# Attention weights times values: one group of eight matmuls per head in place of two groups of four and eight

## The chip, the cores and the metric

The kernel runs on one core of a Trainium2 chip. A core has TensorE (PE in the profile; its weight loads have a row of their own, PEld), VectorE (DVE), ScalarE (ACT), GpSimd (POOL) and the DMA queues that SyncE (SP) and POOL issue. The metric is the device time of one execution in microseconds (us); the figure compared is the median over runs.

## The reference, cut to what matters

The reference is a two-layer decoder trunk on 512 tokens of width 1024, in float32. Each layer is a half-step feed-forward block, a mixer of three parallel head groups, and a second half-step feed-forward block. The change touches only the third head group, causal "forgetting" attention with 8 heads of dimension 64:

```python
def block(i):                                   # one query tile of 128 tokens
    s = einsum('bhqd,bhkd->bhqk', qb, kh) + (cb[..., :, None] - cum[..., None, :])
    s = where(qpos[:, None] >= kpos[None, :], s, MASK_VALUE)
    p = softmax(s, axis=-1)
    return einsum('bhqk,bhkd->bhqd', p, vh)     # weights times values
o = lax.map(block, arange(seqlen // 128))       # four query tiles
```

With 512 tokens there are four query tiles i and four key tiles j, and only the ten blocks with j <= i are not masked: four for j = 0, three for j = 1, two for j = 2, one for j = 3.

## The kernel before, in words

**Precision.** Float32 accuracy is kept by splitting each operand into a high part (type fp32r) and a low part, the remainder. ACT casts the high part, DVE subtracts it from the source to make the low part, and PE multiplies the parts separately.

**The layer.** `ffn`, `mix`, `ffn`, twice. Inside `mix` the attention (`fox_attend`) is a generator that is advanced step by step. Between its steps another generator, `rest`, is advanced: the last value projection, the short convolution's projections and most of the output projection. Its pieces of 9 or 12 matmuls of 512 columns (lines 451 to 458 and 536) are called "the work beside" here. The tuple `BESIDE` says how many pieces go before each attention step. Nearly all PE instructions of this stage are tied into one chain (`follow("p", ...)`; in `fox_attend` the helper `E` does this), so PE's order is the order of the program text. ACT's and DVE's order in the attention is left to the framework's scheduler, which takes ready instructions in the order of the text.

**Steps.** `steps` runs over (head h, p) with h = 0..7 and p = 0, 1, where p = 0 means query tiles 0 and 1 and p = 1 means query tiles 2 and 3. So a layer has 16 steps; the even-numbered ones have p = 0. In step k the kernel runs, in this order:

- `turn(h, p)` transposes the step's weight blocks on PE (line 1843; 3 blocks for p = 0, 7 for p = 1) into PSUM banks "pt", casts the high parts on ACT (1848, tile PH) and subtracts the low parts on DVE (1849, tile PL). Each step has its own PH and PL of seven blocks, two buffers each.
- For p = 0, `prep(h + 2)` transposes and splits a later head's queries and keys (1769 to 1780).
- `scores(steps[k + 2])` writes mask and query-key products into the PSUM banks "sc" (1804), then takes row maxima on DVE (1820), exponentials on ACT (340), a reciprocal (1822) and the scaling to weights (1826 on ACT, 1828 on DVE). There are two "sc" banks, used in turn: p = 0 takes one and p = 1 takes two, so the second bank that a p = 1 step writes is the one that the p = 0 step before it used.
- `values(steps[k - 1])` multiplies the previous step's turned blocks with the head's values V (1861). V holds a head's high and low part side by side, so the 128 output rows are 64 rows of products with the high part and 64 with the low part. The output goes to the single PSUM bank "po".

For p = 0 `values` runs four matmuls: key tile 0 with 256 columns and key tile 1 with 128, each for PH and PL. For p = 1 it runs eight: key tiles 0, 1, 2 with 256 columns and key tile 3 with 128. After p = 1 ACT copies the lower 64 rows out (1874) and DVE adds the upper 64 (1880; for the last head also 1879). The sums feed the last two rows of the output projection, at the end of the stage (line 559 and the lines around it).

Of the kernel before, what the change touches and what calls it, by code (L numbers as in the profile page):

```python
# [9 lines left out]
F32R = mybir.dt.float32r  # L10
# [17 lines left out]
P = 128  # L28
# [35 lines left out]

SKEW_HELD, SKEW_MOVING = 16, 48
EPS = 1e-6
CH = 64
NCH = T // CH
HD = 64
NH = 8  # L70
# [140 lines left out]
class Trunk:  # L211
# [8 lines left out]
    def __init__(self, ctx, tc):  # L220
# [25 lines left out]
        self.epsc = self.const.tile([P, 1], F32, tag="epsc", name="epsc")  # L246
        nc.vector.memset(self.epsc, EPS)
        self.xT = self.res.tile([P, KD, T], F32, tag="xT", name="xT")
# [3 lines left out]
    def build_consts(self, scratch):  # L252
# [16 lines left out]
        nc.vector.memset(self.smask, 1.0)  # L269
        nc.vector.memset(self.smask.rearrange("p (c t) -> p c t", t=CH)[:, :, 0:1], 0.0)  # L270
        self.identb = c.tile([P, P], BF16, tag="identb", name="identb")
# [3 lines left out]

        self.lmask = c.tile([P, 6, CH], U8, tag="lmask", name="lmask")
        self.same = c.tile([P, CH], F32, tag="same", name="same")
        ft = scratch(I32)[:, :P]
# [6 lines left out]
        for i in (  # L285
# [3 lines left out]
            self.tc.add_manual_dep(i.ins, self.first_rows, NOSYNC, reason="opening order")  # L289
        xf = scratch(F32)[:, :CH]  # L290
        later = scratch(F32)[:, : P + CH]
        later, own = later[:, :P], later[:, P:]
# [328 lines left out]
    def rsqrt(self, out, v, r, t):  # L621
# [4 lines left out]
            ("v", nc.vector.scalar_tensor_tensor(  # L626
                out=t, in0=v, scalar=EPS, in1=t, op0=ALU.add, op1=ALU.mult
            )),
# [1154 lines left out]
    def fox_attend(self, pool, half, g):  # L1783


        nc = self.nc
        tl = lambda tag, n: pool.tile([P, T], F32, tag=tag, name=self.n(tag), bufs=n)
        E = lambda i: self.follow("p", i)
        ops, weights, turned = {}, {}, {}

        def prep(h):
            ops[h] = self.fox_prep(pool, h, half[h // 4], g)

        def scores(h, p):
            QA, QB, KA, KB = ops[h]
            pb = pool.tile([P, (384, 896)[p]], F32, tag=f"P{p}", name=self.n("P"), bufs=2)
            s2 = lambda tag: pool.tile([P, 2], F32, tag=tag, name=self.n(tag), bufs=2)
            nm, rs = s2("nm"), s2("rs")
            if p == 0:
                b = self.bank("sc")  # L1800
                at = [b[:, :P], b[:, P : 3 * P]]
            else:
                at = [self.bank("sc")[:, : 3 * P], self.bank("sc")]
            mm = lambda *a, **k: E(nc.tensor.matmul(*a, skip_group_check=True, **k))  # L1804
            if p == 0:
                masked = [b.rearrange("p (b t) -> p b t", t=P)[:, ::2, :]]
            else:
                masked = [at[u][:, (2 + u) * P : (3 + u) * P] for u in range(2)]
            for m in masked:
                mask = self.maskb.unsqueeze(1).to_broadcast([P, 2, P]) if p == 0 else self.maskb  # L1810
                mm(m, self.identb, mask, start=True, stop=False)
            for u in range(2):
                i = 2 * p + u
                c, n = slice(i * P, (i + 1) * P), (i + 1) * P
                mm(at[u], QA[:, c], KA[:, :n], start=False, stop=False)
                mm(at[u], QB[:, c], KB[:, :n], start=False, stop=True)
            to = [pb[:, :P], pb[:, P:]] if p == 0 else [pb[:, : 3 * P], pb[:, 3 * P :]]
            for u in range(2):
                o = slice(u, u + 1)
                nc.vector.tensor_reduce(nm[:, o], at[u], axis=AX.X, op=ALU.max, negate=True)  # L1820
                self.act(to[u], at[u], AF.Exp, bias=nm[:, o], accum_out=rs[:, o])
            nc.vector.reciprocal(rs, rs)
            for u in range(2):
                o = slice(u, u + 1)
                if p:
                    nc.scalar.activation(to[u], to[u], AF.Copy, scale=rs[:, o])
                else:
                    nc.vector.tensor_scalar(to[u], to[u], scalar1=rs[:, o], scalar2=None, op0=ALU.mult)
            weights[h, p] = to

        def turn(h, p):


            to = weights.pop((h, p))
            blocks = [(j, u) for j in range(2 * p + 2) for u in range(2) if j <= 2 * p + u]
            PH, PL = (
                pool.tile([P, 7, P], F32R, tag=t_, name=self.n(t_), bufs=2) for t_ in ("PH", "PL")
            )
            for a in range(0, len(blocks), 4):
                some = blocks[a : a + 4]  # L1840
                tb = self.bank("pt")
                for k, (j, u) in enumerate(some):
                    E(nc.tensor.transpose(
                        tb[:, k * P : (k + 1) * P], to[u][:, j * P : (j + 1) * P], self.ident
                    ))
                ph, pl = (x[:, a : a + len(some), :].rearrange("p b t -> p (b t)") for x in (PH, PL))
                t = tb[:, : len(some) * P]
                nc.scalar.copy(ph, t)
                nc.vector.tensor_sub(pl, t, ph)
            turned[h, p] = blocks, PH, PL  # L1850

        def values(h, p):
            blocks, PH, PL = turned.pop((h, p))
            if p == 0:
                self.ob = self.bank("po")
            last = 2 * p + 1
            for j in range(last + 1):
                at = [k for k, (jj, _) in enumerate(blocks) if jj == j]
                o = slice((2 * p + 2 - len(at)) * P, (2 * p + 2) * P)
                for part in (PH, PL):  # L1860
                    E(nc.tensor.matmul(
                        self.ob[:, o], half[2][:, j, h].rearrange("p a d -> p (a d)"),
                        part[:, at[0] : at[-1] + 1, :].rearrange("p b t -> p (b t)"),
                        start=j == 0 and part is PH, stop=j == last and part is PL,
                        skip_group_check=True,
                    ))
            if p == 0:
                return
            r = slice(64 * (h % 2), 64 * (h % 2) + 64)
            if h % 2 == 0:  # L1870
                self.fo = tl("fo", 1)
            fo = self.fo
            ft = tl(self.tt, self.tb)
            nc.scalar.copy(ft[r, :], self.ob[64:, :])
            if h == NH - 1:

                kt = 4 + h // 2
                nc.scalar.copy(self.yh[kt][:64, :], fo[:64, :])
                nc.vector.tensor_add(self.yh[kt][r, :], self.ob[:64, :], ft[r, :])
            nc.vector.tensor_add(fo[r, :], self.ob[:64, :], ft[r, :])  # L1880
            if h % 2:
                kt = 4 + h // 2
                if h < NH - 1:
                    nc.scalar.copy(self.yh[kt], fo)
                nc.vector.tensor_sub(self.yl[kt], fo, self.yh[kt])

        steps = [(h, p) for h in range(NH) for p in range(2)]
        prep(0)
        yield
        scores(0, 0)  # L1890
        prep(1)
        yield
        scores(0, 1)
        yield
        for k, (h, p) in enumerate(steps):
            turn(h, p)
            if p == 0 and h + 2 < NH:
                prep(h + 2)
            if k + 2 < len(steps):
                scores(*steps[k + 2])  # L1900
            if k:
                values(*steps[k - 1])
            yield
        values(*steps[-1])


    def turn_x(self, res, banks):
# [136 lines left out]
```

## Time and profile before

| | |
|---|---|
| median of 3 runs | 1750.8 us (1749.13 to 1750.95) |
| profiled execution, span from first to last instruction | 1747.5 us |
| PE busy | 1742.1 us, 100% of the span |
| DVE busy | 1415.7 us, 81% |
| ACT busy | 1015.0 us, 58% |
| the values matmuls (line 1861) | 192, with 192 weight loads |
| steps of the attention, layer 0 | 459.5 to 548 us |
| steps of the attention, layer 1 | 1323 to 1411 us |

No separate time of the profiled execution is given beyond its span; the median lies 3.3 us above the span.

How to read the rows: a matmul's duration in the trace holds the pipeline's depth, so a row of 0.28 us may stand for an instruction that holds PE for 0.12 us. What an instruction takes from a busy PE is the distance from its start to the next one's start. In the timeline the columns are the start, the duration, the engine, the line, the operation, output<-inputs, the shape (rows * columns of the held operand, then the moving operand's shape), and the count; a bracket is idle time and what ended it.

### The profile page before, as it was taken

How to read it: one execution, taken by the hardware profiler on the slowest of the kernel's cores; microseconds unless marked ns; L12 is line 12 of the kernel's file. 1: busy time of each engine (PE TensorE's matmuls, PEld its weight loads, DVE VectorE, ACT ScalarE, POOL GpSimd, SP SyncE). 2: the span in 40 equal slices, each digit the busy share in tenths (PEclk: the TensorE clock that was granted, in tenths of full speed). 3: DMA queues.
4: the chain of work that ended last, by engine and by line, in shares of the span. 5: the costliest groups of instructions: out<-in, count | busy, mean ns of one | idle time of the engine just before them, and what ended most of it. 6: DMA issues, size and time to landing. Idle time of an engine off the chain costs nothing.

```text
span 1747.5 us, 33342 instructions
## 1 busy us (share of the span) xinstructions
PE 1742.1 (100%) x13615; PEld 1643.9 (94%) x13615; DVE 1415.7 (81%) x1907; ACT 1015.0 (58%) x1406; POOL 177.0 (10%) x174
## 2 busy tenths in 40 slices
PE   9999999999999999999999999999999999999999
PEld 7999999888888999999989999998888989999998
DVE  7988788678787898888688888876878779888793
ACT  5565565465766565566455656555657665655652
POOL 0011120100000112012001111201000000120200
PEclk9999999999999999999999999999999999999999
DMA  7768784243542876868277787923445447787762
GB/s 213 190 144 194 189 173 107 73 127 92 140 124 89 234 164 152 210 158 170 85 197 165 179 185 180 186 74 80 109 109 144 115 127 196 163 180 190 166 137 97
DMA packets 257449, 262.34 MB, mean 150 GB/s; under 512 B 25816, under 2 KB 236512, under 8 KB 257296
## 3 DMA queue, kind: packets, MB, share of 16 engines
q1 hardware_dynamic: 201440, 192.02, 37.1%
q0 software_dynamic: 55840, 68.19, 24.3%
q8 instruction: 107, 1.75, 0.4%
q14 instruction: 46, 0.38, 0.1%
q10 hardware_dynamic: 16, 0.00, 0.0%
HBM read 226.15 MB, written 2.17 MB: 131 GB/s over the span
## 4 chain that ended last, share of the span: by engine, by line
PE 95%; DVE 2%; issue 2%; DMA 1%; ACT 0%; POOL 0%; SPq 0%; DVEq 0%; POOLq 0%; ACTq 0%
PE mm L451 11%; PE mm L458 11%; PE mm L457 11%; PE mm L536 9%; PE pt L451 6%; PE pt L457 6%; PE pt L458 6%; PE sc L458 6%; PE sc L451 6%; PE sc L457 6%; PE po L451 3%; PE po L457 3%; PE po L458 3%; PE po L536 2%; PE sc L1804 1%
## 5 line engine op out<-in xcount | busy, mean ns | idle before, releaser
L964 DVE TENSOR_TENSOR hl<-w,hl 128x1024 fp32r<-128x1024 f32 x279 | 340.9, 1223 | 89.8 <-ACT hl L962 88.2
L962 ACT CAST hl<-w 128x1024 fp32r<-128x1024 f32 x279 | 293.0, 1050 | 198.0 <-PE mm L458 55.3
L438 DVE TENSOR_TENSOR hl<-st,hl 128x1024 fp32r<-128x1024 f32 (+3 forms) x152 | 159.7, 1053 | 97.4 <-ACT hl L432 96.5
L432 ACT CAST hl<-st 128x1024 fp32r<-128x1024 f32 (+3 forms) x151 | 137.3, 912 | 147.8 <-PE po L458 40.0
L458 PE MATMUL mm<-xc,hl 128*128 128x256 f32 x696 | 191.6, 275 | 0.1
L451 PE MATMUL mm<-xc,hl 128*128 128x256 f32 x698 | 191.6, 275 | 0.0
L457 PE MATMUL mm<-xc,hl 128*128 128x256 f32 x696 | 191.5, 275 | 0.0
L451 PE MATMUL pt<-xc,hl 128*128 128x256 f32 x546 | 149.7, 275 | 0.0
L457 PE MATMUL pt<-xc,hl 128*128 128x256 f32 x544 | 149.7, 275 | 0.0
L458 PE MATMUL pt<-xc,hl 128*128 128x256 f32 x544 | 149.6, 275 | 0.0
L458 PEld LDWEIGHTS mm<-xc,hl 128*128 128x128 f32 x696 | 133.6, 192 | 0.5 <-DVE hl L964 0.5
L451 PEld LDWEIGHTS mm<-xc,hl 128*128 128x128 f32 x698 | 133.9, 192 | 0.1
L457 PEld LDWEIGHTS mm<-xc,hl 128*128 128x128 f32 x696 | 133.6, 192 | 0.0
L451 PE MATMUL sc<-xc,hl 128*128 128x256 f32 (+1 forms) x466 | 127.8, 275 | 0.7 <-DVE u L1085 0.7
L458 PE MATMUL sc<-xc,hl 128*128 128x256 f32 x464 | 127.8, 275 | 0.0
L457 PE MATMUL sc<-xc,hl 128*128 128x256 f32 x464 | 127.7, 275 | 0.0
L536 PE MATMUL mm<-hl,x 128*128 128x512 f32 x432 | 107.4, 384 | 0.0
L451 PEld LDWEIGHTS pt<-xc,hl 128*128 128x128 f32 x546 | 104.7, 192 | 0.0
L457 PEld LDWEIGHTS pt<-xc,hl 128*128 128x128 f32 x544 | 104.4, 192 | 0.0
L458 PEld LDWEIGHTS pt<-xc,hl 128*128 128x128 f32 x544 | 104.4, 192 | 0.0
L451 PE MATMUL mm<-x,hl 128*128 128x512 f32 x272 | 104.4, 384 | 0.0
L458 PE MATMUL mm<-x,hl 128*128 128x512 f32 x272 | 103.1, 379 | 0.0
(529 smaller groups left out, 5464.6 us busy)
## 6 DMA issues: line engine op xcount, KB each, us to landing
w<-in_ffn_w_in_dram SPq DMA_DIRECT2D x124, 512.0 KB, 5.4
w<-in_ffn_w_out_dram POOLq DMA_DIRECT2D x50, 512.0 KB, 9.7
w<-in_ffn_w_out_dram SPq DMA_DIRECT2D x49, 512.0 KB, 4.4
st<-in_ffn_w_out_dram SPq DMA_DIRECT2D x39, 512.0 KB, 3.6
st<-in_w_mix_in_dram SPq DMA_DIRECT2D x72, 256.0 KB, 3.1
st<-in_ffn_w_in_dram SPq DMA_DIRECT2D x71, 256.0 KB, 3.3
w<-in_ffn_w_in_dram POOLq DMA_DIRECT2D x29, 512.0 KB, 9.3
w<-S POOLq DMA_DIRECT2D x29, 512.0 KB, 5.1
```

Source lines behind the costliest of these rows:

```text
L432: a = nc.scalar.copy(hi, src[:, c : c + w])
L438: b = nc.vector.tensor_sub(lo, src[:, c : c + w], hi)
L451: i = nc.tensor.matmul(acc[:, c], ah, bh[:, c.start // 2 : c.stop // 2, :], start=first and c.start == 0, stop=False, skip_group_check=True,)
L457: nc.tensor.matmul(acc, ah, bl, start=False, stop=False, skip_group_check=True)
L458: i = nc.tensor.matmul(acc, al, bh, start=False, stop=last, skip_group_check=True)
L536: self.follow("p", self.nc.tensor.matmul(acc, *((w, woven(x)) if toks is None else (x[:, toks], woven(w))), start=k == 0 and id(acc) not i ...
L962: A(nc.scalar.copy(hi, src))
L964: return lambda: V(nc.vector.tensor_sub(lo, src, hi))
L1804: mm = lambda *a, **k: E(nc.tensor.matmul(*a, skip_group_check=True, **k))
```

## The change

Each head now has one PH and one PL tile of ten blocks, allocated in the p = 0 step, one buffer each. The blocks are ordered by key tile, and within a key tile by query tile in the order 0, 2, 3, 1 (`COLUMNS`), so that the blocks of one key tile are contiguous and their output columns are contiguous in PSUM: 512 columns for key tile 0, 384 for key tile 1, 256 for key tile 2, 128 for key tile 3. `values` runs once per head with eight matmuls instead of twice with four and eight. It runs at the start of the next head's p = 0 step, ahead of that step's `turn`, no longer behind `scores`; the p = 1 steps have no `values`.

`turn` makes the same transposes, and the same number of casts and subtractions with the same sizes, but groups the blocks differently (3; 4 and 3) and writes them with strides into the ten-block tile. Since the output columns stand in the order 0, 2, 3, 1, each final add is split into two adds of 256 columns that put them back in order.

```diff
+COLUMNS = (0, 2, 3, 1)
+PLACES = tuple((j, i) for j in range(4) for i in COLUMNS if i >= j)
+TURNS = (
+    (((0, 0), (0, 1), (1, 1)),),
+    (((0, 2), (0, 3), (1, 2), (1, 3)), ((2, 2), (2, 3), (3, 3))),
+)
...
-            blocks = [(j, u) for j in range(2 * p + 2) for u in range(2) if j <= 2 * p + u]
-            PH, PL = (
-                pool.tile([P, 7, P], F32R, tag=t_, name=self.n(t_), bufs=2) for t_ in ("PH", "PL")
-            )
-            for a in range(0, len(blocks), 4):
-                some = blocks[a : a + 4]
+            if p == 0:
+                turned[h] = [
+                    pool.tile([P, 10, P], F32R, tag=t_, name=self.n(t_)) for t_ in ("PH", "PL")
+                ]
+            for some in TURNS[p]:
                 tb = self.bank("pt")
...
+                at = [PLACES.index(x) for x in some]
+                t = tb[:, : len(some) * P].rearrange("p (b t) -> p b t", t=P)
+                if len(at) == 4:
+                    t = t.rearrange("p (j b) t -> p j b t", b=2)
+                    ph, pl = (
+                        x[:, at[0] : at[0] + 6].rearrange("p (j b) t -> p j b t", b=3)[:, :, :2]
+                        for x in turned[h]
+                    )
+                else:
+                    ph, pl = (x[:, at[0] : at[-1] + 1 : at[1] - at[0]] for x in turned[h])
                 nc.scalar.copy(ph, t)
                 nc.vector.tensor_sub(pl, t, ph)
...
+        def values(h):
+            parts = turned.pop(h)
+            self.ob = self.bank("po")
+            for j in range(4):
+                at = [n for n, (jj, _) in enumerate(PLACES) if jj == j]
+                o = COLUMNS.index(PLACES[at[0]][1])
+                for part in parts:
                     E(nc.tensor.matmul(
-                        self.ob[:, o], half[2][:, j, h].rearrange("p a d -> p (a d)"),
-                        part[:, at[0] : at[-1] + 1, :].rearrange("p b t -> p (b t)"),
-                        start=j == 0 and part is PH, stop=j == last and part is PL,
+                        self.ob[:, o * P : (o + len(at)) * P],
+                        half[2][:, j, h].rearrange("p a d -> p (a d)"),
+                        part[:, at[0] : at[-1] + 1].rearrange("p b t -> p (b t)"),
+                        start=j == 0 and part is parts[0], stop=j == 3 and part is parts[1],
                         skip_group_check=True,
                     ))
...
+            def add(to):
+                for n, b in ((0, slice(0, 4, 3)), (2, slice(1, 3))):
+                    three = lambda x: x.rearrange("p (b t) -> p b t", t=P)
+                    nc.vector.tensor_add(
+                        three(to)[:, n : n + 2], three(self.ob[:64, :])[:, b], three(ft[r, :])[:, b]
+                    )
...
-                nc.vector.tensor_add(self.yh[kt][r, :], self.ob[:64, :], ft[r, :])
-            nc.vector.tensor_add(fo[r, :], self.ob[:64, :], ft[r, :])
+                add(self.yh[kt][r, :])
+            add(fo[r, :])
...
         for k, (h, p) in enumerate(steps):
+            if p == 0 and h:
+                values(h - 1)
             turn(h, p)
             if p == 0 and h + 2 < NH:
                 prep(h + 2)
             if k + 2 < len(steps):
                 scores(*steps[k + 2])
-            if k:
-                values(*steps[k - 1])
             yield
-        values(*steps[-1])
+        values(NH - 1)
```

More of the change, by code (lines that the diff above doesn't have):

```diff
@@ L1841, in turn @@
+            for some in TURNS[p]:
                 tb = self.bank("pt")
-                for k, (j, u) in enumerate(some):
+                for k, (j, i) in enumerate(some):
                     E(nc.tensor.transpose(
-                        tb[:, k * P : (k + 1) * P], to[u][:, j * P : (j + 1) * P], self.ident
+                        tb[:, k * P : (k + 1) * P], to[i - 2 * p][:, j * P : (j + 1) * P], self.ident
                     ))
-                ph, pl = (x[:, a : a + len(some), :].rearrange("p b t -> p (b t)") for x in (PH, PL))
@@ L1847, in turn @@
-                t = tb[:, : len(some) * P]
+                at = [PLACES.index(x) for x in some]
[8 more added lines that the diff above has]
+                    ph, pl = (x[:, at[0] : at[-1] + 1 : at[1] - at[0]] for x in turned[h])
@@ L1848, in turn @@
                 nc.scalar.copy(ph, t)
                 nc.vector.tensor_sub(pl, t, ph)
[L1850 to L1860, printed above, removed]
+        def values(h):
[5 more added lines that the diff above has]
+                for part in parts:
@@ L1865, in values @@
+                        start=j == 0 and part is parts[0], stop=j == 3 and part is parts[1],
                         skip_group_check=True,
                     ))
-            if p == 0:
-                return
             r = slice(64 * (h % 2), 64 * (h % 2) + 64)
```

## The prediction

> **What bounds the kernel now.** I read the page first (busy shares, clock, chain), then the attention's PE timeline, then the DVE and ACT timelines at the places where PE's order would change.
>
> ```profile
> PE 1742.1 (100%) x13615; PEld 1643.9 (94%) x13615; DVE 1415.7 (81%) x1907; ACT 1015.0 (58%) x1406; POOL 177.0 (10%) x174
> PEclk9999999999999999999999999999999999999999
> PE 95%; DVE 2%; issue 2%; DMA 1%; ACT 0%; POOL 0%; SPq 0%; DVEq 0%; POOLq 0%; ACTq 0%
> ```
>
> PE is busy all the time at full granted clock, and the chain that ends last is 95% PE. So the kernel's time is PE's instruction stream: whatever leaves that stream leaves the time, unless PE then waits. A window of layer 0's attention says the same of the stage: 26.00 us of 26.00 for PE, while DVE and ACT have room.
>
> ```profile
> core 0: us, PE busy (x) PEld busy (x) DVE busy (x) ACT busy (x) POOL busy (x), PEclk, DMA share, GB/s
> 455.00:481.00 26.00, 26.00 (x160) 23.32 (x159) 18.42 (x39) 19.12 (x43) 1.55 (x3) 1.00 0.51 132
> ```
>
> **What the values matmuls cost now.** The next fence is the PE timeline of one head: first the p = 0 group and the work beside behind it, then the p = 1 group.
>
> ```profile
> 475.09 0.29 PE L1861 MATMUL po<-PH,V 128*128 128x256 f32 x1
> ...
> 475.51 0.43 PE L451 MATMUL mm<-x,hl 128*128 128x512 f32 x1
> 475.78 0.38 PE L457 MATMUL mm<-x,hl 128*128 128x512 f32 x1
> ...
> 477.94 0.38 PE L458 MATMUL mm<-x,hl 128*128 128x512 f32 x1
> ...
> 479.50 0.28 PE L1861 MATMUL po<-PH,V 128*128 128x256 f32 x1
> 479.62 0.28 PE L1861 MATMUL po<-PL,V 128*128 128x256 f32 x1
> ...
> 480.21 0.22 PE L1861 MATMUL po<-PH,V 128*128 128x128 f32 x1
> 480.27 0.27 PE L1861 MATMUL po<-PL,V 128*128 128x128 f32 x1
> 480.38 0.43 PE L451 MATMUL mm<-x,hl 128*128 128x512 f32 x1
> 480.65 0.38 PE L457 MATMUL mm<-x,hl 128*128 128x512 f32 x1
> ```
>
> Read the starts. A 256-column matmul takes 0.12 us (479.50 to 479.62). The two of 128 columns are marked 0.06 and 0.11 apart, but the 512-column matmul behind them then takes 0.27 us (480.38 to 480.65) where the next ten take 0.216 each (475.78 to 477.94): PE is still waiting for weights there. So the pair really costs 0.06 + 0.11 + 0.05 = 0.22 us, 0.11 each. That 128 columns cost nearly as much as 256 says that below some 0.11 us the weight load is the limit, not the columns. A head costs (475.78 - 475.09 - 0.216) + (480.65 - 479.50 - 0.216) = 0.474 + 0.934 = 1.41 us (0.216 is the 512-column matmul's own).
>
> **What they cost after.** The columns are the same (2560 a head); four matmuls and four weight loads go, two of them of the 128-column kind that pays for a load. The trace holds the new shapes in the same order elsewhere: `fox_decay` multiplies fp32r parts from contiguous rows, 512, 384, 256, 128 columns, each twice, into one bank.
>
> ```profile
> 390.11 0.39 PE L1669 MATMUL pt<-utri,flh 128*8 128x512 f32 x1
> 390.34 0.40 PE L1669 MATMUL pt<-utri,fll 128*8 128x512 f32 x1
> 390.58 0.33 PE L1669 MATMUL pt<-utri,flh 128*8 128x384 f32 x1
> 390.75 0.33 PE L1669 MATMUL pt<-utri,fll 128*8 128x384 f32 x1
> 390.92 0.28 PE L1669 MATMUL pt<-utri,flh 128*8 128x256 f32 x1
> 391.04 0.28 PE L1669 MATMUL pt<-utri,fll 128*8 128x256 f32 x1
> 391.15 0.22 PE L1669 MATMUL pt<-utri,flh 128*8 128x128 f32 x1
> ```
>
> Pairs: 0.47 us for 512 columns, 0.34 for 384, 0.23 for 256. Their held operand has only 8 columns, so no 128-column load limits them; for the last pair I therefore take the 0.22 us measured above, and 0.24 for the 256 pair, as line 1861 itself has it. Sum 0.47 + 0.34 + 0.24 + 0.22 = 1.27 us. The gain is 1.41 - 1.27 = 0.14 us a head, over 16 heads **2.2 us**.
>
> Bounds. From above: if the new matmuls ran like the work beside (0.216 for 512 columns and in proportion 0.162 and 0.108), a head costs 0.43 + 0.32 + 0.22 + 0.22 = 1.19 and 0.22 x 16 = 3.5 us go. From below: the slowest long matmuls of the stage are those of the scores,
>
> ```profile
> 474.62 0.39 PE L1804 MATMUL sc<-A 128*128 128x512 f32 x1
> 474.85 0.40 PE L1804 MATMUL sc<-kb,kb 66*128 66x512 f32 x1
> ```
>
> 0.23 and 0.24 us (474.62 to 474.85 to 475.09); with 0.24, 0.18, 0.12 and 0.11 a head costs 1.30 and 1.8 us go. I take `fox_decay`'s price: contiguous operand and shapes are the nearest.
>
> [...]
>
> **The parts that move or grow.** Transposes, casts and subtractions stay as many and as large; strides on blocks of 128 contiguous elements I cost at nothing, between -0.05 and +0.05 us each on ACT and DVE, where neither bounds the stage. The final add becomes two:
>
> ```profile
> L1849 DVE TENSOR_TENSOR PL<-pt,PH x48: 536/557/692, 460.6 to 1409.0; 128x384 fp32r<-128x384 f32 x32, 128x512 fp32r<-128x512 f32 x16
> L1880 DVE TENSOR_TENSOR fo<-po,t x16: 673/683/685, 472.7 to 1413.7; 64x512 f32<-64x512 f32 x16
> ```
>
> 128 columns are worth 692 - 557 = 135 ns, so a 256-column add is about 683 - 270 = 0.41 us and the two 0.82: +0.14 us on DVE for each of 18 adds, 2.5 us in all, hidden in DVE's idle quarter (18.42 busy of 26.00 us). At the stage's end the output projection's own work stands ahead of the last head's result, and the values' end moves later together with that work; I cost it at nothing.
>
> No DMA is added or moved on SP or POOL; `prep`'s six small DMAs stay behind the same transposes, which come 0.8 us later in the even steps (1.27 ahead of them, 0.47 gone).
>
> **Waits.** Values now stand first in an even step, nearer to their PL. The tightest place is step 1 to step 2 of each layer:
>
> ```profile
> 466.55 1.15 DVE L1849 TENSOR_TENSOR PL<-pt,PH 128x512 fp32r<-128x512 f32 x2
> ...
> 468.24 0.49 PE L1843 MATMUL pt<-ident,P 128*128 128x128 f32 x3
> ```
>
> PL is done at 467.70. PE would begin the values at 468.24 less the 0.47 us group gone from step 1, at 467.77: just after it, and PL is first needed by the second matmul, 0.23 us later. No wait. One buffer for PH and PL makes none either: their next writers wait for transposes that PE runs behind the values.
>
> The place that does get tight is the second "sc" bank of a p = 1 step. Between the scores of an even step and those of the odd one 0.93 us of values disappear. In steps 2 and 4 of each layer only one piece of work beside (12 matmuls) stands between, in nearly all later steps two or 18 matmuls (`BESIDE`); the fence has step 2, with ACT's copy as it falls now:
>
> ```profile
> 472.10 0.58 ACT L1874 COPY t<-po 64x512 f32<-64x512 f32 x1
> 472.11 0.43 DVE L1820 TENSOR_REDUCE nm<-sc 128x1 f32<-128x256 f32 x1 [0.53 <-ACT P L340]
> 472.71 0.47 ACT L340 ACTIVATE P<-sc,nm 128x256 f32<-128x256 f32 x1
> 474.10 0.28 PE L1804 MATMUL sc<-maskb,identb 128*128 128x128 bf16 x2
> ```
>
> The bank's last reader ends at 473.18, the mask matmul starts at 474.10: 0.92 us of room. In the new order PE arrives at 474.10 - 0.47 (step 1's group) - 0.93 (this step's group) + 1.27 (the new group, now ahead) = 473.97. Before the last reader now come the copy (0.58 us on ACT) and the adds (0.82 us on DVE), which came behind or between. If the engines' idle time takes them in, such as the 0.53 us in front of the reduction, the reader still ends by 473.5 and nothing waits; if DVE's adds are passed on in full, it ends at 474.00; if copy and adds are both passed on, at 474.58 and PE waits 0.6 us. So 0 to 0.6 us a place, nothing below zero. I take 0.1, because the middle case lands within 0.03 us of PE; at four places (steps 3 and 5, two layers) **0.4 us**.
>
> **Sum.** -2.2 + 0.4 = -1.8 us on a span of 1747.5: 1745.7, and with the 3.3 us that the median has beyond the span 1749.0 us. A measurement of this kernel can tell about 0.2%, 3.5 us, from no change; so this is a small gain inside that.
>
> **The rivals.**
>
> A, the forecast: 2.2 us of PE work gone, tenths given back, 1747.3 to 1750.8. Chance 0.46.
>
> B, slower: the "sc" bank's wait decides. Place: the mask matmul of the p = 1 scores in steps 3 and 5 of both layers; everything on PE queues behind it. If DVE puts, beside the adds, one long subtraction of the work beside ahead of the reduction,
>
> ```profile
> 474.62 1.23 DVE L438 TENSOR_TENSOR hl<-st,hl 128x1024 fp32r<-128x1024 f32 x1 [0.56 <-ACT hl L432]
> ```
>
> the reader ends at 474.58 + 1.23 = 475.81 and PE waits 1.84 us a place, 7.4 in all: 1750.8 - 2.2 + 7.4 = 1756.0. The kernel is slower than before from 0.56 us a place, and by over 0.2% from 1.43. For it: DVE and ACT work in turns on this chain, and their order is the scheduler's. Against it: the subtraction waits for its own cast, and DVE idles 7.6 us of 26. [...] Chance 0.27, of which 0.15 beyond 0.2%.
>
> C, clearly faster: the long matmuls run at the work beside's rate and no bank waits: -3.5 us. The scores of step 2 also have a hitch, in each layer, of 0.27 - 0.11 = 0.16 us that a later start may remove,
>
> ```profile
> 469.12 0.30 PE L1804 MATMUL sc<-A 128*128 128x128 f32 x1
> 469.39 0.30 PE L1804 MATMUL sc<-kb,kb 66*128 66x128 f32 x1
> ```
>
> another 0.3: 1747.0. For it: 512 columns do take 0.216 us in the work beside. Against it: in `fox_decay` they do not. [...] Chance 0.23.
>
> D, nothing: the loads are hidden after all and only columns count, which are equal. 1750.8. Against it speak the 0.27 us rows. Chance 0.04.
>
> **How the numbers follow.** The predicted time is A's, 1749.0. Faster by over 0.2% is C, 0.23; slower is B's far part, 0.15; within is the rest, 0.46 + 0.12 + 0.04 = 0.62. The range takes in C to 1746.0 and B up to 1754.3, which leaves out B's far part and a little below, under 0.2. A's own range is 1747.3 to 1750.8.
>
> **What would show it.** Line 1861: 128 matmuls instead of 192; starts within a head 0.235, 0.17, 0.12 apart; a head 1.27 us. DVE: 36 adds of about 0.41 us. PE gaps, if any, before line 1804 in steps 3 and 5. I am wrong if line 1861's matmuls wait for PL, if the mask matmul waits more than 0.5 us, or if the reordered ACT and DVE delay the casts of the work beside.

## The result and the profile after

The changed kernel takes 1756.0 us (median of 5 runs, 1753.64 to 1757.28) against 1749.15 us for the kernel before in the same comparison: the ratio is 1.0034, 95% interval 1.0023 to 1.0045. It is slower, by 6.85 us from median to median (5.8 from mean to mean), where a gain of 1.8 us was forecast, and its time lies above the stated range. The kernel before lies 1.65 us under the 1750.8 that the prediction started from. Lines of the changed file stand 8 lower in the helpers and some 18 lower behind the attention; in the rows below L1872 is the values matmul, L1812 the scores, L1828 the row maxima, L348 the exponentials, L1884 the copy, L1889 the adds.

The page of the changed kernel, busy shares and the chain by engine:

```profile
PE 1743.1 (99%) x13551; PEld 1642.8 (94%) x13551; DVE 1414.3 (81%) x1925; ACT 1015.9 (58%) x1406; POOL 177.1 (10%) x174
PE 93%; DVE 4%; ACT 1%; issue 1%; DMA 1%; SPq 0%; ACTq 0%; DVEq 0%
```

There are 64 matmuls and 64 weight loads fewer, as the change says. But PE's share has fallen to 99% and 5% of the chain now run over DVE and ACT: PE waits. Its waits in the changed kernel, longest first (total us, times, longest):

```profile
PE sc L1812 <- ACT P L348: 6.8, 6, 1.9
PE po L1984 <- PEq L2047: 0.8, 1, 0.8
PE pt L1849 <- DVE b L1781: 0.5, 2, 0.3
```

The first row is new, and larger than the 4.5 us that even the shortest run lost: six times, in steps 3, 5 and 9 of each layer, the scores' mask matmul waits for an exponential (0.36, 1.86 and 1.18 us in layer 0; 0.33, 1.86 and 1.18 in layer 1). The second is the start of the kernel, 0.8 us before and after; the third is a short wait of step 3's transposes. What the merged group itself costs, in the PE timeline of one head:

```profile
478.46 0.40 PE L1872 MATMUL po<-PH,V 128*128 128x512 f32 x1
478.69 0.39 PE L1872 MATMUL po<-PL,V 128*128 128x512 f32 x1
478.92 0.34 PE L1872 MATMUL po<-PH,V 128*128 128x384 f32 x1
479.10 0.34 PE L1872 MATMUL po<-PL,V 128*128 128x384 f32 x1
479.27 0.28 PE L1872 MATMUL po<-PH,V 128*128 128x256 f32 x1
479.40 0.28 PE L1872 MATMUL po<-PL,V 128*128 128x256 f32 x1
479.52 0.22 PE L1872 MATMUL po<-PH,V 128*128 128x128 f32 x1
479.57 0.28 PE L1872 MATMUL po<-PL,V 128*128 128x128 f32 x1
479.69 0.51 PE L1849 MATMUL pt<-ident,P 128*128 128x128 f32 x3
```

From 478.46 to 479.69 are 1.23 us, and some 0.02 us more show in the transposes behind. Against 1.41 us before, 0.16 us a head and 2.5 us in all left PE's stream. They were more than given back here, in step 5 of layer 0 (PE timeline):

```profile
484.41 0.22 PE L1812 MATMUL sc<-maskb,identb 128*128 128x128 bf16 x1
486.49 0.22 PE L1812 MATMUL sc<-maskb,identb 128*128 128x128 bf16 x1 [1.86 <-ACT P L348]
```

The first mask goes into the p = 1 step's own bank; the second needs the bank that step 4's scores still hold, and stands for 1.86 us. What DVE did meanwhile, from the end of step 4's values at 479.8 on:

```profile
481.47 0.75 DVE L1889 TENSOR_TENSOR fo<-po,t 64x256 f32<-64x256 f32 x2 [2.04 <-ACT t L1884]
482.25 0.56 DVE L1863 TENSOR_TENSOR PL<-pt,PH 128x384 fp32r<-128x384 f32 x1
482.73 0.74 DVE L1781 SCALAR_TENSOR_TENSOR b<-pt,qkg,b 128x512 fp32r<-128x512 f32 x1
483.39 0.68 DVE L1903 TENSOR_TENSOR fyl<-fo,fyh 128x512 fp32r<-128x512 f32 x1
483.99 0.28 DVE L1828 TENSOR_REDUCE nm<-sc 128x1 f32<-128x128 f32 x1
484.19 0.68 DVE L1396 TENSOR_TENSOR cu<-mm,iv 128x512 f32<-128x512 f32 x1
484.79 0.42 DVE L1828 TENSOR_REDUCE nm<-sc 128x1 f32<-128x256 f32 x1
```

and ACT:

```profile
479.60 1.24 ACT L1834 ACTIVATE P<-P,rs 128x384 f32<-128x384 f32 x2
480.86 0.58 ACT L1884 COPY t<-po 64x512 f32<-64x512 f32 x1
...
484.30 0.37 ACT L348 ACTIVATE P<-sc,nm 128x128 f32<-128x128 f32 x1 [1.27 <-DVE nm L1828]
484.57 0.19 ACT L348 ACTIVATION_READ_ACCUMULATOR P<-sc,nm 128x1 f32 x1
484.66 0.82 ACT L440 CAST hl<-st 128x768 fp32r<-128x768 f32 x1
485.38 0.59 ACT L1862 CAST PH<-pt 128x512 fp32r<-128x512 f32 x1
485.86 0.48 ACT L348 ACTIVATE P<-sc,nm 128x256 f32<-128x256 f32 x1
```

Read them as one chain. The values are done at 479.8, but ACT is busy with two scalings until 480.8 and copies only then. DVE's next instruction is the adds, which need the copy, so DVE stands still for 2.04 us. Five instructions (the two adds and three others) then pass before the first maximum at 483.99, although step 4's scores were complete at about 481.2. The second maximum follows only after the first exponential has begun and something of the work beside (L1396) is put in between; the second exponential then stands behind two casts on ACT. It ends at 486.3, and PE has been at the mask since 484.4.

The profiled run (1757.28 us) has one more part. In two stretches of 3.4 us PE's granted clock is half (0.50 from 1260.2 to 1263.2 and from 1355.8 to 1358.8), one of them right behind the wait of 1.86 us in layer 1:

```profile
core 0: us, PE busy (x) PEld busy (x) DVE busy (x) ACT busy (x) POOL busy (x), PEclk, DMA share, GB/s
1354.00:1355.50 1.50, 1.06 (x6) 0.97 (x6) 1.50 (x5) 1.38 (x4) 0.00 (x0) 1.00 0.86 204
1355.50:1359.00 3.50, 3.50 (x11) 2.75 (x10) 3.27 (x7) 1.50 (x5) 0.57 (x1) 0.52 0.35 114
```

In that stretch the work beside's matmuls start 0.43 us apart (1355.99, 1356.42, 1356.84), behind it 0.216 (1359.22 to 1360.30); eight of them make 1.7 us, an estimate from these starts. Two of the five runs have a mean clock of 0.998 and take 1757.0 and 1757.3 us; the two shortest have 1.000 and take 1753.6 and 1753.8. The median run, 1756.0, has 1.000 too, so the clock does not explain all of the spread. The balance of the profiled run against the span of before is: waits 6.8 + 0.5, half clock 3.4, merging -2.5, and one wait of 0.7 us for a DVE result in the second feed-forward block that the profiled run of before had and this one has not: +7.5 of the 8.0 us that the spans differ by.

### The profile page after: what moved, and what is told of

Read it like the earlier page. It is cut to its first block, busy times and chain, and to the rows that moved or that the text cites. A ratio compares the mean times of both kernels' runs of the same rounds, so it can differ in the third digit from the quotient of the medians.

```text
span 1755.5 us, 33238 instructions
## 1 busy us (share of the span) xinstructions
PE 1743.1 (99%) x13551; PEld 1642.8 (94%) x13551; DVE 1414.3 (81%) x1925; ACT 1015.9 (58%) x1406; POOL 177.1 (10%) x174
## 4 chain that ended last, share of the span: by engine, by line
PE 93%; DVE 4%; ACT 1%; issue 1%; DMA 1%; SPq 0%; ACTq 0%; DVEq 0%
PE mm L459 10%; PE mm L466 10%; PE mm L465 10%; PE mm L544 9%; PE pt L459 6%; PE pt L465 6%; PE pt L466 6%; PE sc L466 6%; PE sc L459 6%; PE sc L465 6%; PE po L459 3%; PE po L465 3%; PE po L466 3%; PE po L544 2%; PE sc L1812 1%
```

## The experiments

Theory W: merging gains about 2.4 us of PE time, and what is lost is the wait for the second "sc" bank, made by the order in which ACT and DVE now work. Rival S: the new tile's shape (strided casts, one buffer, split adds) is at fault. Rival D: only the distance on PE between two scores groups, from which 0.93 us of values went. "Before" in the tables is the kernel before on the same chip as the run.

| kernel | median us | before us | ratio (95%) | PE's wait at the scores, us (times) |
|---|---|---|---|---|
| the change | 1756.0 | 1749.15 | 1.0034 (1.0023 to 1.0045) | 6.8 (6) |
| e1 merged, behind the scores | 1751.1 | 1749.99 | 1.0007 (0.9998 to 1.0016) | 0.5 (2) |
| e2 copy and adds behind the scores | 1755.9 | 1749.99 | 1.0035 (1.0022 to 1.0048) | 0.5 (2) |
| e3 before, values first | 1758.26 | 1749.99 | 1.0050 (1.0037 to 1.0062) | 6.1 (6) |
| e4 before, split adds | 1749.67 | 1749.99 | 1.0001 (0.9992 to 1.0010) | none |
| e5 change, second mask later | 1750.36 | 1749.27 | 1.0004 (0.9996 to 1.0013) | 1.4 (2) |
| e6 e2, but head 3 early | 1754.49 | 1749.27 | 1.0029 (1.0020 to 1.0039) | 4.3 (4) |
| e7 e6 with e5's mask | 1752.08 | 1749.27 | 1.0014 (1.0005 to 1.0023) | 3.0 (2) |
| e8 change, copy on DVE | 1751.08 | 1749.27 | 1.0011 (1.0002 to 1.0020) | 3.8 (4) |
| e9 change, both maxima first | 1747.78 | 1749.51 | 0.9986 (0.9977 to 0.9995) | none |
| e10 e9 with e8's copy | 1750.07 | 1749.51 | 1.0003 (0.9994 to 1.0012) | 2.6 (2) |
| e11 before, both maxima first | 1749.5 | 1749.51 | 1.0000 (0.9991 to 1.0008) | none |

### e1: the merged group behind the scores

```diff
-            if p == 0 and h:
-                values(h - 1)
             turn(h, p)
+            if p:
+                split(h, p)
...
                 scores(*steps[k + 2])
+            if p == 0:
+                if h:
+                    values(h - 1)
+                split(h, p)
```

`split` is the half of `turn` with the casts and subtractions; for p = 0 it has to come behind `values`, because the ten-block tile has a single buffer.

> The merged group of eight matmuls is kept, with the ten-block tile, the strided writes and the split adds; it stands behind the step's scores, where the old p = 1 group stood, and the p = 0 step's casts into the single-buffered tile come behind it. Theory W (the loss is the wait for the second sc bank, made by moving the values and their copy and adds ahead of the scores): no PE wait at the scores' mask matmul, the 0.15 us a head of PE work stay gained, 1749.2 - 2.4 = 1746.8 us, between 1746 and 1748. Rival S (the new tile makes it slow: strided casts, one buffer, two adds instead of one): 1753 or more, as the changed kernel. Rival D (only the 0.93 us that no longer stand between two scores groups on PE count): 1746.8, since the distance is back.

Measured 1751.1 us: neither 1746.8 nor 1753. The bank's wait is nearly gone with the whole new tile in place, which speaks against S, but the 2.4 us were not kept. PE's waits of this kernel behind the start:

```profile
PE mm L544 <- ACT cyh L1416: 0.7, 2, 0.4
PE pt L1847 <- DVE rs L1830: 0.5, 2, 0.3
PE sc L1812 <- ACT P L348: 0.5, 2, 0.2
```

In place of one large wait there are several small ones, for a cast of the work beside, for a reciprocal, for the bank (the two waits left at the scores are at an even step's bank, not at the second bank of a p = 1 step). My theory had only the bank; it missed that ACT and DVE have other due times as tight. These waits are not the whole difference. The first matmul on the tile `m` (line 457, here 465), ahead of all that was changed, starts at 104.52 us in this profiled run and at 102.88 before; in e2 it is 105.53 and in e3 104.92. No run here says why.

### e2: matmuls first, copy and adds behind the scores

```diff
             if k + 2 < len(steps):
                 scores(*steps[k + 2])
+            if p == 0 and h:
+                finish(h - 1)
```

`finish` is the part of `values` behind the matmuls.

> The changed kernel with its eight matmuls first in the step, as they are; only the copy and the adds (and what follows from them) are written behind the scores. Theory W, with the order of ACT and DVE as the cause: the mask matmul waits at most 0.2 us a place, 1747.0 to 1748.5 us. Rival D (the lost distance on PE alone): the waits stay near 4 us a layer, 1753.6 to 1757. Rival S: the same as the changed kernel, 1753.6 to 1757.

Measured 1755.9 us, the figure that D and S named; but the trace says why:

```profile
PE mm L544 <- ACT fyh L1904: 3.9, 2, 2.0
PE po L1989 <- PEq L2052: 0.8, 1, 0.8
PE sc L1812 <- ACT P L348: 0.5, 2, 0.3
```

PE's order, and so the distance, is the changed kernel's, and the bank's wait fell from 6.8 to 0.5 us. So D falls, and so does S: the order of ACT and DVE made that wait. W had the wait right and the time (1747.0 to 1748.5) wrong: the time did not fall, because now the output projection waits 2 us in each layer for head 3's cast, whose copy and adds were put off, and four of the five runs have a mean clock of 0.998, where all of e1's have 1.000: 0.2% of the profiled run's 1755.7 us is 3.5 us, by estimate two stretches of 1.7 us.

### e3: the kernel before with its groups first

```diff
+            if k:
+                values(*steps[k - 1])
             turn(h, p)
...
-            if k:
-                values(*steps[k - 1])
```

> The kernel before, with its two groups of four and eight matmuls, its two buffers and its single adds, but each group moved to the start of its step. Theory W: no PE work is gained; the copy and the add stand ahead of the reductions as in the changed kernel, and the four-matmul group still gives 0.47 us of distance, so the waits are those of the changed kernel less 0.47 us each: about 0.1, 1.5 and 0.9 us a layer, 5 us in all, 1754 us (1752 to 1756). Rival S: 1749, nothing of the tile is changed. Rival D: 1749, since 0.92 and 0.80 us of room cover the 0.46 us of distance lost.

```profile
PE sc L1804 <- ACT P L340: 6.1, 6, 1.7
```

Six waits, the longest 1.73 us where 1.5 was expected, with not one matmul merged and nothing of the tile changed. S and D expected 1749. The time, 1758.3, is above W's 1752 to 1756, in which it was already counted that no PE work is saved. The profiled run and three others have a mean clock of 0.998, which W did not count, but the median run has 1.000, so part of the excess stays open.

### e4: the split adds alone

```diff
-            nc.vector.tensor_add(fo[r, :], self.ob[:64, :], ft[r, :])
+            for c in (slice(0, 2 * P), slice(2 * P, 4 * P)):
+                nc.vector.tensor_add(fo[r, c], self.ob[:64, c], ft[r, c])
```

> The kernel before with each final add done as two adds of 256 columns, nothing else. Theory W and rival D: 1749 us, within 1 us, since DVE has room where the adds stood. Rival S: slower by 2 us or more, 1751 and up.

1749.67 against 1749.99: nothing, as W and D expected. S is out for the adds too.

### e5: the second mask later

```diff
-            for m in masked:
+            for m in masked[:1]:
...
             for u in range(2):
+                if p and u:
+                    mm(masked[1], self.identb, self.maskb, start=True, stop=False)
```

> The changed kernel; in a p = 1 step the mask matmul into the second sc bank stands behind the first bank's two products, not ahead of them, so PE reaches that bank 0.44 us later (264 + 180 ns, the two products of 384 columns). Theory W: every wait before that mask gets shorter by up to 0.44 us (0.36 to 0, 1.86 to 1.4, 1.18 to 0.75 us, twice), 2.4 us less: 1753.5 us, between 1751 and 1755, and what is left still ends with an exponential before that mask. Rival (PE waits there for something else that merely shows as the bank, such as the first bank or the operands): waits and time unchanged, 1755 to 1757.

```profile
PE sc L1812 <- ACT P L348: 1.4, 2, 0.7
```

1750.4 us, below the 1751 to 1755 that W gave. The two waits left are those of step 9, 0.69 us each, which is 1.18 less 0.49, as the dose says; ACT's and DVE's order there is the changed kernel's. In step 5 the wait went altogether, where 1.4 us should have stayed. There the scheduler also put the copy ahead of the two scalings (480.59 and 481.20 in its ACT timeline), so that DVE stood still for 0.44 us before the adds, not 2.04, and the second exponential ahead of the casts of PH, where the change has it behind one. So a reorder of 0.44 us on PE moved the other engines' order as well, and the experiment is no pure dose.

### e6 and e7: head 3's result early, then also the mask later

```diff
             if p == 0 and h:
                 values(h - 1)
+                if h == 4:
+                    finish(3)
...
-            if p == 0 and h:
+            if p == 0 and h and h != 4:
                 finish(h - 1)
```

> The second experiment (eight matmuls first, copy and adds behind the scores), but for head 3 alone, whose result the output projection takes up in the same step, copy and adds stand right behind the matmuls. Theory: the projection's wait of 1.95 us for head 3's cast goes in both layers, and the bank's wait in step 9 comes back (about 1.2 us), the waits in steps 3 and 5 stay below 0.5 us: 1755.9 - 3.9 + 2.4 = 1754.4, or down to 1751 if the half-clock stretches behind the 1.95 us waits (1.7 us each) go too. Rival (late adds are bad for another reason than that deadline): 1755 to 1757 as in the second experiment.

> The sixth experiment with the fifth's later mask. Theory: the wait in step 9 falls by 0.44 us in both layers and those in steps 3 and 5 go, about 1.5 us less than the sixth: 1750 to 1752. If the parts do not add up, because ACT and DVE then fall behind elsewhere, it stays with the sixth.

```profile
PE sc L1812 <- ACT P L348: 4.3, 4, 1.9
```

That row is e6's. The projection's wait for head 3 is gone in both layers, which confirms the due time, and the bank's wait in step 9 is back with 1.9 us (1.2 expected); 1754.5 us as forecast. In e7 step 9's wait is 1.5 us, the others are gone, 1752.1 us, just above what was forecast. (One of e7's eleven runs took 3658 us; nothing here gives a reason. The median of the other ten is 1751.8.) For step 8 there is thus no good place in the text as long as the maxima stand apart: adds early make the bank late, adds late make the projection late.

### e8: the copy on DVE

```diff
-            nc.scalar.copy(ft[r, :], self.ob[64:, :])
+            nc.vector.tensor_copy(ft[r, :], self.ob[64:, :])
```

> The changed kernel with the copy of the lower 64 rows on DVE in place of ACT, so that DVE's adds no longer wait for ACT's queue (2.04 us idle in step 4, 1.31 in step 8). Theory W in its form 'DVE stands still behind a copy that is late on ACT': adds start 1.3 us sooner and cost 0.68 us more, the waits in steps 5 and 9 fall by about 0.7 us: 1756 - 3 = 1753 (1751 to 1755). Rival 'DVE has too much work': one more DVE instruction of 0.68 us a head makes the waits longer, 1757 or more.

```profile
PE sc L1812 <- ACT P L348: 3.8, 4, 1.1
```

DVE has 0.7 us a head more to do and the kernel is 5 us faster than the change, at the lower edge of the forecast. So too much work on DVE was not the trouble. Step 5's wait fell from 1.86 to 0.76 us and step 3's went, which fits DVE standing behind a copy that was late on ACT; step 9's stayed at 1.13 us where a fall of 0.7 was expected, so there the copy alone does not decide.

### e9 to e11: both maxima before both exponentials

```diff
             for u in range(2):
                 o = slice(u, u + 1)
                 nc.vector.tensor_reduce(nm[:, o], at[u], axis=AX.X, op=ALU.max, negate=True)
+            for u in range(2):
+                o = slice(u, u + 1)
                 self.act(to[u], at[u], AF.Exp, bias=nm[:, o], accum_out=rs[:, o])
```

e9 is the changed kernel with this alone, e10 has e8's copy besides, e11 is the kernel before with this alone.

> The changed kernel with one change in the scores: both row maxima stand ahead of both exponentials, so that on DVE the second reduction of a p = 0 step follows the first at once and nothing long comes between them. Values, copy and adds stay first in the step. Theory (the bank is late because its second reduction waits for the first exponential and lets adds, casts and the work beside pass): the bank's last reader ends 0.6 to 1.5 us sooner, the waits in steps 3 and 9 go, that in step 5 is at most 0.7 us; 0 to 1.4 us left over both layers, 1749.3 - 2.4 + (0 to 1.4) = 1746.9 to 1748.3 us. Rival (the moved values starve DVE and ACT as a whole, whatever their order): the waits only move, 1751 or more.

> The ninth with the copy on DVE as in the eighth. If the ninth has already no wait left, the added 0.68 us a head on DVE does nothing or harms: 1747 to 1749. If the ninth still waits for ACT's copy in step 5, this is faster than the ninth by up to 1.4 us.

> The control: the kernel before with both row maxima ahead of both exponentials, nothing else. PE waits for no bank there, so theory: unchanged, 1749.3 within 1 us. If this alone is faster by 2 us, the ninth's gain is not the merging's.

e9 takes 1747.78 us: faster than the changed kernel and than the kernel before (0.9986, interval 0.9977 to 0.9995). Its DVE in the stretch that was shown for the changed kernel, step 4 of layer 0:

```profile
480.56 0.75 DVE L1891 TENSOR_TENSOR fo<-po,t 64x256 f32<-64x256 f32 x2 [0.60 <-ACT t L1886]
481.34 0.62 DVE L1828 TENSOR_REDUCE nm<-sc 128x1 f32<-128x128 f32 x2
482.33 0.69 DVE L1905 TENSOR_TENSOR fyl<-fo,fyh 128x512 fp32r<-128x512 f32 x1 [0.37 <-ACT fyh L1904]
```

its ACT, and all its waits on PE:

```profile
479.95 0.58 ACT L1886 COPY t<-po 64x512 f32<-64x512 f32 x1 [0.18 <-PE pt L1851]
480.56 1.23 ACT L1836 ACTIVATE P<-P,rs 128x384 f32<-128x384 f32 x2
...
483.28 0.37 ACT L348 ACTIVATE P<-sc,nm 128x128 f32<-128x128 f32 x1
483.53 0.21 ACT L348 ACTIVATION_READ_ACCUMULATOR P<-sc,nm 128x1 f32 x1
483.62 0.48 ACT L348 ACTIVATE P<-sc,nm 128x256 f32<-128x256 f32 x1
```

```profile
PE po L1986 <- PEq L2049: 0.8, 1, 0.8
PE sc L465 <- DVE m L900: 0.2, 1, 0.2
```

The maxima stand together (x2) right behind the adds, the exponentials follow each other on ACT, the last reader ends at 484.1 instead of 486.3, and no wait at the scores is left. The values and the adds are those of the changed kernel, and so is PE's order. In step 4, however, the scheduler moved a second thing: the copy stands ahead of the two scalings, and DVE stood still for 0.60 us, not 2.04. So for step 5's wait e9 does not separate the two orders, and e5 (with its mask 0.44 us later) and e2, which have the copy ahead of the scalings but the maxima apart, wait there only 0 and 0.26 us. Step 9's wait is the clean case. In step 8 the copy follows the scalings in both kernels, DVE's idle time before the adds is 1.31 us in both and the first maximum comes 3.13 us behind the copy's start in both; only the second maximum now follows at once, and the wait of 1.18 us is gone.

e11, the control, is 1.0000: the order of the maxima alone is worth nothing where PE does not wait for the bank, so what e9 gains over before comes with the merging. Of the 2.5 us saved, 1.7 reached the median. The profiled runs show 1.2 of it where the change is: from `fox_decay`'s first matmul to the first matmul on `xc` behind the attention (390.11 to 600.23 us before) e9 is 0.5 us shorter in layer 0 and 0.75 in layer 1. Another 0.9 us lies behind that point in layer 1, where before waits 0.67 us for a DVE result and e9 does not; no experiment ties that to the merging. Part of the rest is lost at step 5's transposes, in pieces too short for the list of waits:

```profile
483.14 0.38 PE L466 MATMUL mm<-x,hl 128*128 128x512 f32 x1
483.64 1.21 PE L1851 MATMUL pt<-ident,P 128*128 128x128 f32 x7
484.68 0.28 PE L1812 MATMUL sc<-maskb,identb 128*128 128x128 bf16 x2
```

From the first of these rows to the last are 1.54 us, and 0.98 for the same rows of before (482.81 to 483.79). Without that delay PE would have come to the mask at about 484.1, just when the last reader ends: the bank is free in time, but with no room.

e10 missed: with the copy on DVE the scheduler put the maxima apart again (481.20 and 482.65 in its DVE timeline) and the bank's wait of 1.3 us in step 5 came back.

## Why the prediction was wrong, point by point

- **PE's price of the group** was right. 1.27 us a head were forecast from `fox_decay`'s rows; 1.23 to 1.25 were measured, with 0.23, 0.17 and 0.12 us for the long shapes. The work beside's rate, rival C's, would have had 0.216 for 512 columns; the trace has 0.23 (478.46 to 478.69), so `fox_decay` was the better model. The reading that weight loads limit the 128-column pair has its rows in before's trace: a `128*128` load takes 0.19 us, the loads there start 0.11 apart (480.22, 480.33, 480.44), and the one for the matmul at 480.65 ends at 480.63; `fox_decay`'s `128*8` loads take 0.09. No run changed the loads alone.
- **The adds** were right in size and effect: 36 of 0.41 us, and e4 shows that in the kernel before they cost nothing.
- **No wait for PL, none for the single buffer**: right; no row of the changed kernel shows either.
- **The second "sc" bank: "I take 0.1" at "four places"**: this is the step that failed. Measured were about 0.35, 1.86 and 1.18 us in each layer, 6.8 in all against 0.4, and at six places: step 9, which I let go because 18 matmuls stand ahead of it, is one of them. The mechanism and the place were named, in the term and in rival B, with B's price of 1.84 us a place for the case that work beside gets ahead of the reduction; what was wrong is the weight between the cases.
- **Why it was mis-sized**, as the runs show it. I followed one place, step 2 to step 3, and there the 0.36 us lie inside the 0 to 0.6 that I gave; the error was to carry it to step 5 and to let step 9 go. I had moved the copy and the adds ahead of a chain whose links stay together. But a p = 0 step's chain is maximum, exponential, maximum, exponential across ACT and DVE, and at each link the scheduler let others pass: in step 4 the copy on ACT behind two scalings, five DVE instructions ahead of the first maximum, one between the two, two casts on ACT ahead of the last exponential. With the maxima together (e9) all six waits go; in step 9 that is the only order that differs, in step 5 the copy's place differs too. The row of before with the bracket "0.53 <-ACT P L340" on the second maximum showed that break, and I counted it as idle time that could take in work.
- **The idle quarter of DVE** was no cushion. DVE was not short of time (e8 gives it more work and is faster); it stood idle for 2.04 us because its next instruction, the first add, waited for ACT's copy.
- **Not foreseen: the clock.** One of the changed kernel's two waits of 1.86 us was followed by 3.4 us at half clock, and its two longest runs are those with a mean clock of 0.998. That explains why they are the longest, not its loss: its shortest run is still 4.5 us above the median of before.
- **The median** of 1756.0 equals B's figure by chance. B had four waits of 1.84 us on a start of 1750.8; there were two of that size and four smaller ones, and before's median was 1749.15.
- **The 3.3 us beyond the span** mixed the profiled run with a slower median: in the runs on record the time lies 1.7 to 1.9 us above the span of the same run. The forecast gain does not depend on it.

## What to carry to other kernels

When work is moved ahead on the engine that bounds, follow what depends on it on the other engines too: here its copy and adds moved ahead of the links of another chain, and while the adds waited for ACT's copy DVE stood still for 2.04 us, at a busy share of 81%. The chain that alternates between two engines here (maximum, exponential, maximum, exponential) was open at each alternation; with the maxima grouped (e9) the 6.8 us of waits at the scores went, and the order on ACT and DVE, not the saved matmuls, decided whether the merging paid. Look at the timeline of every such edit: under a scheduler an edit of one line moves others too, as e5 and e9 show. Room measured at one place (0.92 us) says nothing on the next if a scheduler makes the order: look for the instruction that it would let in, and price that.

## What the runs showed of the hardware that was not expected

- Two stretches of 3.4 us in the changed kernel's profiled run had half the granted clock, each worth 1.7 us by the estimate above. One came right behind the wait of 1.86 us in layer 1 (1355.6 to 1359.0). Behind the wait of the same length in layer 0 none came: the clock is 1.00 from 486.5 to 493.3. The other stretch (1260.0 to 1263.4) stands behind no wait, PE being busy throughout 1258.0 to 1260.0. What begins such a stretch is not shown.
- The mean clocks of the runs differ with the kernels' longest waits on PE. The change, e2, e3 and e6, whose longest wait is 1.7 to 2.0 us, have runs at 0.998 (2 of 5, 4 of 5, 4 of 5 and 5 of 9). In before and in the other experiments, whose longest wait is 1.5 us or less, no recorded clock is below 0.999. That the length of the wait decides is not shown by this; the median runs of the change and of e3 have 1.000.
- Matmuls on contiguous 512 columns took 0.23 us in the values as in `fox_decay`, those of the work beside, which read their operand in another pattern (two by 256), 0.216. That the pattern is the reason is not shown; no run changed it alone.
